# Two transformer layers on one core: the residual rows go to DRAM during the experts, the norm behind them goes tile by tile, and small products are joined

## The chip, the cores and the metric

The kernel runs on one core of a Trainium2 chip. Times are device microseconds of that core; the figure compared is the median over the runs. One execution was profiled, and all rows below are of that one. Engines are called TensorE (PE in the profile; its weight loads are PEld), VectorE (DVE), ScalarE (ACT), GpSimd (POOL) and SyncE (SP), which issues most loads from DRAM.

## The reference

512 tokens of width 1024 pass two layers in float32.

```
first layer:
  h = rmsnorm(x);  proj = h @ w_in  -> u, v_a, q, k, v_b
  y_a = u * spatial gating(v_a);  y_b = difference attention(q, k, v_b), 8 heads
  merged = sigmoid(gate_a) * (y_a @ w_up_a) + sigmoid(gate_b) * (y_b @ w_up_b)
  x = x + merged @ w_out
  t = rmsnorm(x) * norm2_g
  group and two of its experts for each token (4 groups of 8 experts, width 256)
  x = x + sum over the two chosen experts of c * (silu(t @ w1) * (t @ w3)) @ w2
second layer:
  h = rmsnorm(x) * norm_mix
  compressed, selected and window attention with gates; a convolution of 31 taps;
  attention to a memory of 256 tokens; three gated branches summed; x = x + merged @ w_out
  x = x + (silu(t @ w_gate) * (t @ w_up)) @ w_down,   t = rmsnorm(x) * norm_ffn
```

## The kernel before

**Products.** Most products are made three times, from a high and a low part of both operands (`split_to`, `mm3`, lines 313 to 315): high by high, high by low, low by high. Rounding to the high part is ACT's, the low part is DVE's. Weights come in blocks of 1 MB: loaded (`wraw`), split (`whi`, `wlo`, lines 303 and 304), used. The experts' products and the memory's take weights and operands unsplit (`mraw`, line 272).

**Order of the work.** A queue (`Dense`) holds the dense products in their order, with calls of other functions between them. A step makes one group of products; evacuations (`evac`) are put off to the next group. Other stages (the two attentions) call the queue for so many ns between their own steps. Loads are issued as far ahead as there are places: ring `w` has the two buffers `wraw`, and ring `m`, for the experts and the memory, has places that are granted and taken back by `grant`: eight of the ring `p`, three `q`, the buffers of `w`, `h` and `l` (2 each), `u` and `s`. The instructions of an engine are ordered by a scheduler from the program; inside `ordered(...)` an engine keeps the program's order. Each engine and SP's queue work in that order, so what waits holds up what is behind it.

**Start.** Four tiles of 128 tokens are normed (`norm_in`, line 439 is the product with root and gain), transposed and split (`lay_in`), two of them ahead of the first products.

**Output projection and router (500 to 580 us).** `w_out` comes in four blocks of 256 columns. After each half block `ev_x` adds to the residual rows `x1` (in the buffer `r0`, 16 KB a partition), multiplies the new rows with the gain on POOL (line 803), writes them to DRAM (`xg_d`) and sums squares. `lay_l` transposes and splits the rows, and `logits` multiplies them with the router's weights, high and low (36 columns). The router's chain of small DVE operations follows (lines 1124 to 1232); it ends with the index lists, by which `gather` reads each expert's rows from DRAM.

**Experts (580 to 812 us).** 16 pairs of experts, each with room for 64 tokens. `lay_x` transposes the gathered rows (one half copied by ACT, one by DVE), `push_up` makes the products with w1 and w3 (line 923), `lay_h` the gating, `push_down` the product with w2 (line 943), which is scattered by token and choice to DRAM (`y_d`, line 949). The places are taken back near the end (pairs NP-5 and NP-4).

**Between the layers (812 to 860 us).** Three of four products for the memory's keys and values (line 997) remain. Four tiles `yk` of 1 MB are read from `y_d`, added to `x1` (line 1359), normed for two tiles at a time (squares on ACT, line 1365, ten small DVE steps, product with root and gain, line 1370), transposed and split (`lay_xn`); tiles 2 and 3 are laid between the two halves of the first block of weights. `x1` goes to DRAM (`x2_d`), from where it comes back at the end of the layer.

**Second layer.** The small products that matter here: the compression (`push_cmp`, 2 x 2 blocks of 24 products, 64 columns high and low apart), the gates (`push_gate`, 24 products of 24 columns), and in the sparse attention the products with the compressed values (line 1685), whose probabilities are transposed to 32 rows (line 1704).

Of the kernel before, what the change touches and what calls it, by code (L numbers as in the profile page):

```python
# [6 lines left out]
F32 = mybir.dt.float32  # L7
# [5 lines left out]
OP = mybir.AluOpType  # L13
# [9 lines left out]
RING = 8  # L23
# [136 lines left out]
def _body(ctx, tc, I, out):  # L160
# [4 lines left out]
    def sub(stack, name, bufs=1, side="left", **kw):  # L165
# [11 lines left out]
          "back": {"p": [f"p{i}" for i in range(RING)], "q": [f"q{i}" for i in range(RING2)], "s": ["s0"], "u": ["U"],  # L177
# [181 lines left out]
    def rsqrt(dst, ss, shape, scale, eps, pause=None, after=None):  # L359
# [15 lines left out]
        dve.scalar_tensor_tensor(dst, a, 0.703952253 * 2.38924456 * z, dst, op0=OP.add, op1=OP.mult)  # L375
# [3 lines left out]
        dve.scalar_tensor_tensor(dst, a, 0.703125, dst, op0=OP.add, op1=OP.mult)  # L379

# [44 lines left out]
    xs_in = {}  # L425

# [6 lines left out]
    def norm_in(t):  # L433
# [4 lines left out]
        rsqrt(rr, ss, [128, 1], 1.0 / D, EPS, after=eye)  # L438
        dve.scalar_tensor_tensor(y, xn[:, t], rr, gain, op0=OP.mult, op1=OP.mult)
# [28 lines left out]
    def constants(kp):  # L468
# [37 lines left out]
        pool.affine_select(wsn, wsn, pattern=[[0, 8], [-1, 128]], compare_op=OP.is_ge, fill=0.0, base=0,  # L506
# [51 lines left out]
    with ordered(nc.sync.engine, nc.scalar.engine):  # L558
# [18 lines left out]
        norm_in(3)  # L577
# [212 lines left out]
    xg_d = tc.dram_tile([S, D], F32, name="xg_d")  # L790
# [4 lines left out]
    def ev_x(c, q, ps):  # L795
# [4 lines left out]
        if q == 0:  # L800
            R["xg", c] = R["rt"].tile([128, 4, 256], F32, name="xg", tag="row")
        xg = R["xg", c][:, 2 * q:2 * q + 2]
        pool.tensor_mul(xg, xs, R["g2"][:, cs][:, None, :].to_broadcast([128, 2, 256]))
# [7 lines left out]
        if q:  # L811
            (pool if c == 3 else act).dma_start(xg_d.rearrange("(t p) d -> p t d", p=128)[:, :, cs], R["xg", c])
# [12 lines left out]
    def logits(c, q):  # L825
# [14 lines left out]
    def wo_amid(c):  # L840
        dn.flush()
        lay_l(c, 0)

    def wo_step(c):
        if c:
            logits(c - 1, 1)
        grant((2, 2, 2, 0)[c])

    for c in range(4):
        dense_N(w_out[:, c * 256:c * 256 + 256], 0, 256, lambda: mT, lambda _, q, ps, c=c: ev_x(c, q, ps),  # L850
                between=(lambda c=c: wo_between(c)) if c else None, amid=(lambda c=c: wo_amid(c)) if c else None)
# [15 lines left out]
    def gather(p):  # L867

        pool.indirect_dma_start(out=R["xe"][p % 2], out_offset=None, in_=xg_d,
# [1245 lines left out]
```

## Time and profile before

| | us |
|---|---|
| median of 3 runs | 1728.38 (1727.83 to 1731.09) |
| profiled execution | 1730.11 |
| its span | 1728.4 |
| TensorE busy | 1667.7 (96% of the span) |
| DVE, ACT, POOL busy | 890.9, 650.1, 269.5 |

A row of the timeline gives start, duration, engine, line, operation, output and inputs; equal neighbours are merged (x5), and the duration is then that of all. What stands in square brackets is idle time of the engine ahead of it and what ended it. Products overlap one another on TensorE: the pace is the distance of their starts, not their duration.

### The profile page before, as it was taken

The numbers are of one execution on the slowest core, as the hardware profiler recorded it, in microseconds if no ns is written. First come the engines' busy times: TensorE is split into PE (matmuls) and PEld (weight loads), VectorE is DVE, ScalarE is ACT, GpSimd is POOL, SyncE is SP. The second block draws the span as 40 slices with busy tenths as digits, with TensorE's granted clock in tenths as the row PEclk, the third lists the DMA queues.
The fourth block names the chain that finished last, engine by engine and source line by source line (L and its number), as shares of the span: only waits on it lengthen the run. The fifth ranks groups of instructions, "written<-read, shape, count | busy, mean of one in ns | idle before, by whom it ended". The sixth has DMA issues, their size and how long they took to land.

```text
span 1728.4 us, 24549 instructions
## 1 busy us (share of the span) xinstructions
PE 1667.7 (96%) x9802; PEld 1361.1 (79%) x9802; DVE 890.9 (52%) x1958; ACT 650.1 (38%) x1127; POOL 269.5 (16%) x266
## 2 busy tenths in 40 slices
PE   8999999999999899888899999999999999999999
PEld 8988899998789655455789877777779888888887
DVE  7642358887653412010778755645995544444221
ACT  4221235545523122111435487787433322222111
POOL 2000001101112222111100045454101011111000
PEclk9999999999999999999899999999999999999999
DMA  6323333133458999999434322222243233332241
GB/s 213 98 74 122 122 98 98 53 96 98 152 159 317 355 419 402 422 416 389 179 98 122 122 64 77 86 68 74 91 153 110 74 97 97 98 97 98 70 137 37
DMA packets 146859, 265.98 MB, mean 154 GB/s; under 512 B 11707, under 2 KB 113798, under 8 KB 134198
## 3 DMA queue, kind: packets, MB, share of 16 engines
q1 hardware_dynamic: 128598, 228.42, 36.9%
q0 software_dynamic: 11184, 27.41, 5.3%
q10 hardware_dynamic: 6960, 8.56, 1.4%
q8 instruction: 78, 1.28, 0.3%
q14 instruction: 39, 0.32, 0.1%
HBM read 248.62 MB, written 18.87 MB: 155 GB/s over the span
## 4 chain that ended last, share of the span: by engine, by line
PE 75%; DVE 9%; DMA 8%; ACT 4%; issue 2%; POOL 0%; ACTq 0%; SPq 0%; DVEq 0%; POOLq 0%
PE pd L313 19%; PE pd L315 19%; PE pd L314 18%; DMA mraw<-in_w 4%; PE pd L923 4%; PE pa L396 3%; PE pa L314 2%; PE pa L315 2%; PE pa L313 2%; DMA y_d<-yt,dest 2%; PE pd L943 2%; DVE wlo L304 2%; ACT whi L303 1%; PE pa L1717 1%; PE pa L1699 1%
## 5 line engine op out<-in xcount | busy, mean ns | idle before, releaser
L304 DVE TENSOR_TENSOR wlo<-wraw,whi 128x2048 fp32r<-128x2048 f32 (+3 forms) x113 | 246.4, 2180 | 202.7 <-ACT whi L303 197.5
L303 ACT ACTIVATE whi<-wraw 128x2048 fp32r<-128x2048 f32 (+3 forms) x126 | 213.1, 1697 | 350.0 <-PE pd L314 213.7
L314 PE MATMUL pd<-wlo,hT 128*128 128x256 f32 x512 | 144.5, 282 | 0.7 <-DVE wlo L304 0.5
L313 PE MATMUL pd<-whi,hT 128*128 128x256 f32 x512 | 144.9, 283 | 0.3 <-ACT hT L253 0.2
L315 PE MATMUL pd<-whi,hT 128*128 128x256 f32 x512 | 144.1, 281 | 0.0
L315 PE MATMUL pd<-hnT,wlo 128*128 128x512 f32 x352 | 139.4, 396 | 0.0
L313 PE MATMUL pd<-hnT,whi 128*128 128x512 f32 x352 | 139.3, 396 | 0.0
L314 PE MATMUL pd<-hnT,whi 128*128 128x512 f32 x352 | 139.2, 395 | 0.0
L923 PE MATMUL pd<-mraw,xs 128*64 128x256 f32 x1024 | 122.1, 385 | 17.1 <-DMA mraw<-in_w 16.9
L923 PEld LDWEIGHTS pd<-mraw,xs 128*64 128x64 f32 x1024 | 75.2, 138 | 62.5 <-DMA mraw<-in_w 21.2
L313 PE MATMUL pd<-xnT,whi 128*128 128x512 f32 (+1 forms) x280 | 112.4, 401 | 0.0
L315 PE MATMUL pd<-xnT,wlo 128*128 128x512 f32 (+1 forms) x280 | 111.1, 397 | 0.0
L314 PE MATMUL pd<-xnT,whi 128*128 128x512 f32 (+1 forms) x280 | 110.9, 396 | 0.0
L314 PEld LDWEIGHTS pd<-wlo,hT 128*128 128x128 f32 x512 | 96.8, 189 | 1.7 <-DVE wlo L304 0.7
L313 PEld LDWEIGHTS pd<-whi,hT 128*128 128x128 f32 x512 | 96.8, 189 | 1.1 <-ACT hT L253 0.5
L315 PEld LDWEIGHTS pd<-whi,hT 128*128 128x128 f32 x512 | 96.7, 189 | 0.0
L1826 POOL TENSOR_TENSOR oa<-oa,ctm 128x512 f32<-128x512 f32 x60 | 77.5, 1291 | 99.0 <-ACT ctm L1825 97.1
L891 DVE SCALAR_TENSOR_TENSOR sg<-sg,pd 128x256 f32<-128x256 f32 x16 | 6.7, 421 | 161.1 <-ACT sg L890 161.1
L314 PEld LDWEIGHTS pd<-hnT,whi 128*128 128x128 f32 x352 | 66.1, 188 | 16.1
L313 PEld LDWEIGHTS pd<-hnT,whi 128*128 128x128 f32 x352 | 66.1, 188 | 15.8
L315 PEld LDWEIGHTS pd<-hnT,wlo 128*128 128x128 f32 x352 | 66.1, 188 | 15.8
L313 PE MATMUL pd<-hT,whi 128*128 128x512 f32 x192 | 76.7, 399 | 0.0
(521 smaller groups left out, 3879.2 us busy)
## 6 DMA issues: line engine op xcount, KB each, us to landing
mraw<-in_w SPq DMA_DIRECT2D x96, 1024.0 KB
wraw<-in_w_in SPq DMA_DIRECT2D x43, 1024.0 KB
wraw<-in_w_gate SPq DMA_DIRECT2D x19, 1024.0 KB
wraw<-in_w_up SPq DMA_DIRECT2D x11, 1024.0 KB
wraw<-in_w_down SPq DMA_DIRECT2D x10, 1024.0 KB
wraw<-in_w_out SPq DMA_DIRECT2D x8, 1024.0 KB
wraw<-in_w_up_a SPq DMA_DIRECT2D x4, 1024.0 KB
qk<-qk POOLq DMA_DIRECT2D x16, 256.0 KB, 6.4
```

The source lines that it names most:

```text
L303: act.activation(h[:, sl], r[:, sl], AF.Copy)
L304: (pool if i in by_pool else dve).tensor_tensor(l[:, sl], r[:, sl], raw(h[:, sl]), op=OP.subtract)
L313: pe.matmul(ps, ah, bh, start=start, stop=False)
L314: pe.matmul(ps, ah, bl, start=False, stop=False)
L315: pe.matmul(ps, al, bh, start=False, stop=stop)
L396: pe.transpose(ps[:, t * 128:t * 128 + 128], src_of(t), ident)
L891: dve.scalar_tensor_tensor(sg, sg, 1.0, hid[:, 0:256], op0=OP.add, op1=OP.mult)
L923: pe.matmul(ph[64 * m:64 * m + 64, 256 * j:256 * j + 256], XS[p][:, k, 64 * m:64 * m + 64], w[:, k], start=k == 0, stop=k == 7)
L943: pe.matmul(py[64 * q:64 * q + 64], hs[:, k, own], wt[:, k, 512 * q:512 * q + 512], start=k == 0, stop=k == 1)
L1699: pe.matmul(po[g, qt][64 * x:64 * x + 64], v, p, start=first, stop=last)
L1717: pe.matmul(ps[:, :nm], Q[:, 4 * g + i, qs], KS[:, br, g, x, :nm], start=x == 0, stop=x == 1)
L1826: pool.tensor_add(acc, acc, tm)
```

## The change

- The residual rows, not multiplied with the gain, are written to DRAM (`x1_d`) block by block where `xg_d` was written; the gain is applied by DVE at the transposes of the gathered rows (`lay_x`).
- The buffer `r0` is then room for two more loads ("x"), and the ring `p` has nine places. The buffers of `w` are granted after the third block of `w_out`. The experts' results have three buffers for four, the gated rows one for two.
- Behind the experts the rows are read back (`x1b`), and each tile of 128 tokens is added, squared and normed for itself (`norm_x`): POOL multiplies with the gain, and the root comes in as a diagonal matrix at the transposes. Tile 0 comes ahead of the first products, the others between them. One split of weights fewer comes ahead of it.
- Side by side: the router's weights, high and low in one operand of 100 columns, the compression's blocks in 128, the gates' weights in 56; two products for three, and the halves are summed by a product with stacked identities or by DVE. The compressed probabilities are padded to 128 columns, the compressed values to 128 rows.
- At the start the inverse roots follow one another, and a POOL operation on the spatial weights is put behind the last norm.

```diff
-RING = 8
+RING = 9
@@ ring_tile
+        if at == "x":
+            if "x" not in MR:
+                MR["x"] = r0.tile([128, 2, 8 * 256], F32, name="xroom", tag="r0")
+            return MR["x"][:, tag].rearrange("p (a b) -> p a b", a=shape[1])
@@ dense_N
-                        if q and i and amid:
-                            amid()
+                        if i and amid:
+                            amid(q)
@@ norm_in
-        rsqrt(rr, ss, [128, 1], 1.0 / D, EPS, after=eye)
+        order["rs"] = rsqrt(rr, ss, [128, 1], 1.0 / D, EPS, after=order["rs"])
...
-        norm_in(3)
+        behind(order["wsn"], norm_in(3))
@@ ev_x
-        xg = R["xg", c][:, 2 * q:2 * q + 2]
-        pool.tensor_mul(xg, xs, R["g2"][:, cs][:, None, :].to_broadcast([128, 2, 256]))
...
-            (pool if c == 3 else act).dma_start(xg_d.rearrange("(t p) d -> p t d", p=128)[:, :, cs], R["xg", c])
+            (pool if c == 3 else act).dma_start(x1v[:, :, cs], x1[:, :, cs])
@@ logits
-            mm3(R["lgp", q][0:36, 0:256], R["wrh"][:, k], R["wrl"][:, k], xT[0][:, j], xT[1][:, j],
-                k == 0, k == 7)
+            for x in range(2):
+                pe.matmul(R["lgp", q][0:100, 0:256], R["wrx"][:, k], xT[x][:, j], start=k + x == 0, stop=k + x == 8)
@@ wo_step
+        if c == 2:
+            dn.room["w"] = 0
+            grant(2, "w")
@@ lay_x
-            if q:
-                dve.tensor_copy(xs[:, 4:8], p3)
-            else:
-                act.activation(xs[:, 0:4], p3, AF.Copy)
+            ks = slice(4 * q, 4 * q + 4)
+            dve.tensor_mul(xs[:, ks], p3, R["g2k"][:, ks, None].to_broadcast([128, 4, 128]))
@@ lay_h, push_down: sg bufs 2 -> 1, yt bufs 4 -> 3
@@ experts, p == NP - 4
-            dn.call(lambda: (grant(-RING2, "q"), grant(-1, "s")))
+            dn.call(lambda: (grant(-RING2, "q"), grant(-1, "s"), grant(-2, "x")))
@@ router, after the copies of the logits
+        grant(2, "x")
         dn.prepare(2)
         lgq = psa()
         for t in range(4):
-            pe.transpose(lgq[:, t * 36:t * 36 + 36], lgT[:, t * 128:t * 128 + 128], ident[0:36, 0:36])
+            pe.matmul(lgq[:, t * 36:t * 36 + 36], lgT[:, t * 128:t * 128 + 128], halves2r[0:100], start=True, stop=True)
...
-        pool.dma_start(R["g2"], bc(I["norm_mix_2"], 0, [[0, 128], [1, D]]))
@@ between the layers
     dense_N(w_in2, 2328, 256, lambda: xnT, lambda c, q, ps: ev_qm(c, q, ps),
-            between=lambda: (lay_xn(2), lay_xn(3)))
+            between=lambda: norm_x(2), amid=lambda q: norm_x(3 if q else 1))
...
-    dn.prepare(5)
+    dn.prepare(4)
...
+    x1 = r0.tile([128, 4, D], F32, name="x1b", tag="r0")
+    for t in range(4):
+        sync.dma_start(x1[:, t], x1v[:, t])
+    yk = []
+    for tag in "KQ":
+        y2 = br_p.tile([128, 2, 2, D], F32, name="yk", tag=tag)
+        for i in range(2):
+            yk.append(y2[:, i])
+            sync.dma_start(y2[:, i], yv[:, 2 * (tag == "Q") + i])
+    gx = half("C", "gx", F32)[:, 0:2].rearrange("p a b -> p (a b)")
+    act.dma_start(gx, bc(I["norm_mix_2"], 0, [[0, 128], [1, D]]))
+    dgx = half("D", "dgx", F32)
...
+    def gains(t):
+        act.activation(yk[t][:, 0], x1[:, t], AF.Square, accum_out=nss[:, t:t + 1])
+        order["gx"] = pool.tensor_mul(yk[t][:, 1], x1[:, t], gx)
+
+    def factor(a, b):
+        rsqrt(nrr[:, a:b], nss[:, a:b], [128, b - a], 1.0 / D, EPS)
+        for t in range(a, b):
+            dve.tensor_scalar(dgx[:, t, 0:128], ident, nrr[:, t:t + 1], None, op0=OP.mult)
+
+    def norm_x(t):
+        if t == 0:
+            add_row(0, 0)
+            add_row(0, 1)
+            gains(0)
+            add_row(1, 0)
+            factor(0, 1)
+            add_row(1, 1)
+            gains(1)
+            add_row(2, 0)
+            add_row(3, 0, pool)
+        elif t == 1:
+            factor(1, 2)
+            add_row(2, 1)
+            add_row(3, 1)
+            gains(2)
+            gains(3)
+        elif t == 2:
+            factor(2, 4)
+        ts_ = slice(t * 128, t * 128 + 128)
+        for hf in range(2):
+            ps = transpose4(lambda k: yk[t][:, 1, (4 * hf + k) * 128:(4 * hf + k) * 128 + 128], diag=dgx[:, t, 0:128])
+            ks = slice(4 * hf, 4 * hf + 4)
+            split_to(xnT[0][:, ks, ts_], xnT[1][:, ks, ts_], ps.rearrange("p (k s) -> p k s", k=4))
...
+    with ordered(nc.vector.engine):
+        norm_x(0)
+        dn.step()
+        dn.step()
+    for t in range(4):
+        pool.dma_start(x2_d[:, t], x1[:, t])
@@ push_cmp
-                    mm3(cm["ps"][0:64, 256 * a:256 * a + 256], BH[a][:, 0, jj], BH[a][:, 1, jj], wt[0][:, j], wt[1][:, j],
-                        jj == 0, jj == 15)
+                    for x in range(2):
+                        pe.matmul(cm["ps"][:, 256 * a:256 * a + 256], BH[a][:, jj].rearrange("p x i -> p (x i)"),
+                                  wt[x][:, j], start=jj + x == 0, stop=jj + x == 16)
@@ cmp_gelu
-        act.activation(x, cm["ps"][0:64], AF.Copy)
+        act.activation(x, cm["ps"][64:128], AF.Copy)
+        dve.tensor_add(x, x, cm["ps"][0:64])
@@ push_gate
-                mm3(ps[0:24], wt[0][:, k], wt[1][:, k], xnT[0][:, k], xnT[1][:, k], k == 0, k == 7)
+                for x in range(2):
+                    pe.matmul(ps[0:56], wt[:, k], xnT[x][:, k], start=k + x == 0, stop=k + x == 8)
@@ cmp_turn_
-            ps = transpose4_32(sc)
-            hl = [t2("pt").bitcast(F32R)[0:32] for _ in range(2)]
-            split_to(hl[0], hl[1], ps[0:32])
+            ps = transpose4(lambda i: sc[:, i])
+            hl = [t2("pt").bitcast(F32R) for _ in range(2)]
+            split_to(hl[0], hl[1], ps)
```

## Rows read from the trace of the kernel before

**Rows 1.** The page's first part: busy us, share, instructions of each engine.
```profile
PE 1667.7 (96%) x9802; PEld 1361.1 (79%) x9802; DVE 890.9 (52%) x1958; ACT 650.1 (38%) x1127; POOL 269.5 (16%) x266
```
**Rows 2.** Stretches: us, busy of PE, PEld, DVE, ACT, POOL; clock, DMA share, GB/s.
```profile
540.00:550.00 10.00, 10.00 (x87) 9.96 (x87) 2.08 (x3) 2.90 (x10) 2.53 (x2) 1.00 0.77 288
550.00:560.00 10.00, 9.93 (x85) 9.58 (x84) 3.17 (x6) 2.34 (x8) 2.34 (x3) 1.00 0.42 133
...
570.00:580.00 10.00, 6.37 (x78) 5.82 (x78) 7.78 (x27) 0.32 (x2) 3.29 (x4) 1.00 0.78 300
580.00:590.00 10.00, 9.76 (x86) 6.47 (x86) 3.78 (x15) 1.58 (x3) 1.95 (x2) 1.00 0.79 293
...
720.00:730.00 10.00, 7.79 (x55) 4.25 (x52) 0.95 (x2) 2.06 (x4) 3.04 (x3) 1.00 1.01 421
...
840.00:850.00 10.00, 7.30 (x33) 6.65 (x32) 8.54 (x20) 4.25 (x8) 2.06 (x5) 0.50 0.30 118
```
**Rows 3.** Waits of SP's DMA queue, 500 to 850: total us, times, longest.
```profile
SPq L272 <- PE pd L315: 20.6, 2, 12.9
SPq L272 <- DVE vals L1223: 17.7, 1, 17.7
```
**Rows 4.** Timeline between the experts and the second layer.
```profile
820.85 2.56 SPq L1345 DMA_DIRECT2D yk<-y_d  x4
...
828.22 6.01 DVE L1359 TENSOR_TENSOR x<-x,yk 128x1024 f32<-128x1024 f32 x5
...
838.98 3.65 PE L396 MATMUL pa<-ident,ny 128*128 128x128 f32 x16 [5.71 <-issue]
...
845.32 0.58 PE L313 MATMUL pd<-whi,xnT 128*128 128x256 f32 x1 [2.69 <-ACT xnT L253]
```
**Rows 5.** Timeline of DVE and POOL, at the start and at the router.
```profile
8.79 2.48 DVE L439 SCALAR_TENSOR_TENSOR ny<-xn,nrr,gain 128x1024 f32<-128x1024 f32 x2
...
19.28 1.05 DVE L374 SCALAR_TENSOR_TENSOR rs_a<-rs_a,rs_v 128x1 f32<-128x1 f32 x1
...
559.87 1.29 POOL L803 TENSOR_TENSOR xg<-x,gain 128x512 f32<-128x512 f32 x1
...
560.40 1.68 DVE L366 TENSOR_SCALAR rs_v<-s 128x4 f32<-128x4 f32 x1
```
**Rows 6.** TensorE's waits over the span: total us, times, longest.
```profile
PE pd L923 <- DMA mraw<-in_w: 16.9, 9, 3.0
...
PE pa L396 <- DVE ny L439: 3.7, 2, 2.5
...
PE pa L314 <- DVE xT L822: 1.9, 1, 1.9
...
PE pa L1500 <- DVE cu L1494: 1.1, 1, 1.1
```
**Rows 7.** TensorE's timeline: a logits group to the next product; a compressed value pair.
```profile
545.00 0.28 PE L313 MATMUL pa<-xT,wrh 128*36 128x256 f32 x1
...
545.70 0.28 PE L313 MATMUL pd<-whi,mT 128*128 128x256 f32 x1
...
1056.69 0.73 PE L1685 MATMUL pa<-pt,vcs 32*128 32x512 f32 x2
1057.35 0.39 PE L1717 MATMUL pa<-KS,Q 128*128 128x256 f32 x1
```
**Rows 8.** DMA issues: count, KB each, median us from issue to landing.
```profile
xg_d<-xg POOLq DMA_DIRECT2D x1, 512.0 KB, 8.9
...
y_d<-yt,dest POOLq DMA_INDIRECT x32, 7.5
```
**Rows 9.** Timeline of SP's queue, 545 to 560.
```profile
545.07 14.96 SPq L272 DMA_DIRECT2D mraw<-in_w  x5
```
**Rows 10.** Stretches of the compression's products (24) and of the gates' (24 and 3 more).
```profile
923.55:926.43 2.88, 2.88 (x24) 2.78 (x24) 0.00 (x0) 0.00 (x0) 1.00 0.01 3
...
887.20:892.75 5.55, 5.55 (x27) 2.52 (x24) 5.50 (x7) 2.52 (x7) 0.00 (x0) 1.00 0.02 3
```

More of the change, by code (lines that the diff above doesn't have):

```diff
@@ L176, in _body @@
     MR = {"free": deque(), "owed": {}, "at": {},
-          "back": {"p": [f"p{i}" for i in range(RING)], "q": [f"q{i}" for i in range(RING2)], "s": ["s0"], "u": ["U"],
+          "back": {"p": [f"p{i}" for i in range(RING)], "q": [f"q{i}" for i in range(RING2)], "s": ["s0"], "u": ["U"], "x": [0, 1],
                    "w": ["wraw0", "wraw1"], "h": ["whi0", "whi1"], "l": ["wlo0", "wlo1"]}}
@@ L425, in _body @@
     xs_in = {}
+    order = {"rs": eye}
     def warm(n):
@@ L1103, in _body @@
     pool.memset(ones, 1.0)
+    halves2r = rt.tile([128, 36], F32, name="halves2r")
+    pool.memset(halves2r, 0.0)
+    for at in (0, 64):
+        pool.tensor_copy(halves2r[at:at + 36], ident[at:at + 36, at:at + 36])
     grant(RING - 6)
@@ L1111, in _body @@
     grant(RING2, "q")
-    dn.room["w"] = 0
-    grant(2, "w")
     grant(2, "h")
@@ L1127, in _body @@
         lg = tmp("lg", 4, 36)
[L1128 removed]
+        lgT = rt.tile([100, S], F32, name="lgT", tag="jk", bufs=2)
         for q in range(2):
[L1130 removed]
+            act.activation(lgT[:, 256 * q:256 * q + 256], R["lgp", q][0:100, 0:256], AF.Copy)
+        grant(2, "x")
         dn.prepare(2)
@@ L1353, in half @@
         return (p or br_p).tile([128, 4, S], dtype, name=name, tag=tag)
-    ny = [half(tag, "ny", F32).rearrange("p (a k) s -> p a (k s)", a=2) for tag in "CD"]
-    with ordered(nc.vector.engine):
-        def add_rows(t, ks=(0, 1)):
-            for k in ks:
-                dve.tensor_add(x1[:, t], x1[:, t], yk[t][:, k])
-        for q in range(2):
-            ss, rr = small("nss", [128, 2], 4), small("nrr", [128, 2], 4)
-            for t in (2 * q, 2 * q + 1):
-                add_rows(t, (1,) if t == 2 else (0, 1))
-                act.activation(ny[q][:, t % 2], x1[:, t], AF.Square, accum_out=ss[:, t % 2:t % 2 + 1])
-            if q == 0:
-                add_rows(2, (0,))
-            rsqrt(rr, ss, [128, 2], 1.0 / D, EPS)
-            for t in range(2):
-                dve.scalar_tensor_tensor(ny[q][:, t], x1[:, 2 * q + t], rr[:, t:t + 1], R["g2"], op0=OP.mult, op1=OP.mult)
+    x1 = r0.tile([128, 4, D], F32, name="x1b", tag="r0")
@@ L1395, in _body @@
     kcT = na.tile([128, 2, 2, 32], F32R, name="kcT")
-    vcs = na.tile([32, 2, 2, 64], F32R, name="vcs")
+    vcs = na.tile([128, 2, 2, 64], F32R, name="vcs")
+    pool.memset(raw(vcs), 0.0)
+    scz = [na.tile([128, 4, 128], F32, name=f"scz{i}") for i in range(2)]
+    for z in scz:
+        pool.memset(z, 0.0)
     cmask = na.tile([128, 512], F32, name="cmask")
@@ L1460, in ev_blk @@
     def ev_blk(a, ps):
-        pool.memset(blk[a][:, :, :, 31:32], 0.0)
+        behind(pool.memset(blk[a][:, :, :, 31:32], 0.0), order["gx"])
         for g in range(2):
@@ L1549, in lay_kv, with side @@
             pool.dma_start(KS[other, br, g], KS[own, br, g])
+    halves2 = p2.tile([128, 24], F32, name="halves2")
+    behind(pool.memset(halves2, 0.0), order["gx"])
+    for at in (0, 32):
+        pool.tensor_copy(halves2[at:at + 24], ident[at:at + 24, at:at + 24])
     def push_gate():
         v = w_in2.rearrange("(k p) c -> p k c", p=128)
+        load, split = wtile([(lambda r: r, v[:, :, 1280:1304])], (128, 8, 24))
+        both = p2.tile([128, 8, 56], F32R, name="gboth")
+        behind(pool.memset(raw(both), 0.0), order["gx"])
+        def side(r):
+            h, l = split(r)
+            act.activation(both[:, :, 0:24], raw(h), AF.Copy)
+            act.activation(both[:, :, 32:56], raw(l), AF.Copy)
+            return both
         def g(wt):
@@ L1699, in gather_values @@
                 pe.matmul(po[g, qt][64 * x:64 * x + 64], v, p, start=first, stop=last)
-        def transpose4_32(sc):
-            ps = psa()
-            for i in range(4):
-                pe.transpose(ps[0:32, i * 128:i * 128 + 128], sc[:, i], ident)
-            return ps
         def scores(u, hf, cps):
@@ L1882, in ev_g1 @@
         act.activation(Qb["g1"][:, j], ps, AF.Tanh, scale=0.5)
-    for t in range(4):
-        pool.dma_start(x2_d[:, t], x1[:, t])
-    lay_xn(0)
-    lay_xn(1)
     dn.call(lambda: lay_qm(0))
```

87 lines of the change are left out of this document (40 added, 47 removed).

## The prediction

> **What bounds the kernel now.** I read the busy shares first: TensorE is busy for 96% of the span [rows 1], so in most places only fewer products can shorten it. Then the stretches of 10 us, with the DMA's share beside TensorE's. The reader is to see two gaps in the DMA's work ahead of the experts (0.77 and 0.42 of full from 540 to 560, 0.78 and 0.79 from 570 to 590), and behind them a DMA at 1.01 while TensorE drops to 7.79 of 10 us [rows 2]. The experts run from 580 to 812, and there the weights bound the kernel, not the products: whatever is loaded in the gaps needn't be loaded later. Third, the waits of SP's DMA queue, which say why the gaps are there: no place is free. It waits 20.6 us in two waits for the last products that read old buffers, and 17.7 us for the router to end [rows 3]. Fourth, the timeline between the experts and the second layer: TensorE has been idle for 5.7 us when the transposes of the normed rows start at 838.98, and for 2.7 more when the first product on them starts at 845.32 [rows 4], and the granted clock there is 0.50 [rows 2], the 1.2 GHz level.
>
> **The change, part by part.** Durations are from the profiled execution, which took 1730.11 us (span 1728.4). That is 1.7 us above the median of the runs, 1728.38, so the sum comes off 1730.11 and then 1.7 us more for the median.
>
> *Start.* The inverse roots of the first two row tiles, now interleaved, run one behind the other, so the first norm can start before 8.79; a POOL operation on the spatial weights goes behind the last norm, where a small step of DVE now takes 1.05 us [rows 5]. TensorE waits 3.7 us there in two waits [rows 6]. Between nothing and 3.7 I take 1.5, because the first wait then meets the split of the weights. **-1.5.**
>
> *Router logits.* Three products for each of 16 (column block, half, k) become two, high and low weights side by side in 100 columns. Six go from 545.00 to 545.70 [rows 7], 0.117 us each: 16 x 0.117 = **-1.9**, in a stretch where TensorE is full [rows 2]. The rows now go to DRAM as they are, so POOL's products with the gain go, 1.29 us each; the last of them ran beside the router's first step, which took 1.68 us [rows 5], and TensorE then waited 1.9 us for its next operand [rows 6]. Between 0 and 1.9 I take 1.0, since two POOL fills of the gather's buffers stay. **-1.0.** The gain is applied where the experts' rows are transposed: both halves are then DVE's instead of one ACT's, some 0.7 us more in a pair of experts, and a pair lasts 14.5 us (232 over 16). DVE is nearly empty there (0.95 of 10 us [rows 2]) and the first products need only the first half: nothing. Without that cover it is 16 x 0.7 = 11 us.
>
> *Three more places for weights (one in the ring, two in the room of the residual rows).* Each holds 1.05 MB; at the 421 GB/s of the experts' stretch [rows 2] that is 2.5 us. Free ahead of the experts are 2.3 + 5.8 = 8.1 us in the first gap and 2.2 + 2.1 = 4.3 in the second [rows 2]. The ring's place falls into the first. The room opens when the last store of the rows has landed: that takes 8.9 us [rows 8] from about 559.9, when POOL now starts its last product [rows 5], so at about 569. The five loads that go out from 545.07 on [rows 9] are 12.5 us of DMA and are still landing then; the room's two, 5 us, go into the second gap, which also loses the 0.5 MB of the second layer's gain. Filled: 3 x 2.5 = 7.5 us. Bounds: 2.5 (only the ring's place pays) and 7.5. I take the upper one, since the second gap is about as large as what goes in and the DMA sets the experts' end (from 720 to 730 TensorE is idle for 2.2 us [rows 2], and its longest wait in total is for these weights, 16.9 us [rows 6]). **-7.5.**
>
> *What the places cost.* One buffer less for the experts' results (3 for 4) and for the gated rows (1 for 2). The one reader of the gated rows stands ahead of their next writer: nothing. A result's buffer comes round after one and a half pairs, some 21 us, against 7.5 us to landing [rows 8]; only the last four stand closer, and y is late behind them for another reason, as follows.
>
> *Behind the experts.* Now: y is read from 820.85, five sums run from 828.22, and one chain for two tiles leads to 845.32, 17.1 us later [rows 4]; of the 7.3 us of products at half clock from 840 to 850 [rows 2] half, 3.7, is lost. New: 2 MB of rows are read again and 0.5 MB of gain is loaded late, 2.6 MB or 6 us in front of y in a queue that is full. But the first sum now waits for a split of weights and not for y (no idle is shown ahead of it [rows 4]), and that split moves behind; y's first tile, 2.5 us of DMA from 820.85, can have been there by some 825. So it is some 3 us late against 828.22, and its chain is short: two sums (2.4), square (1.25), ten small steps (2.0), diagonal (0.2), transposes and first copy (1.5), about 8 us instead of 17. The first product comes some 6 us earlier. Then tiles 1 to 3 wait each for its own factor, with a square and a sum ahead of it on ACT and DVE, 1 to 3 us each, where there is no wait now. Between -6 (ACT copies ahead of its squares) and +6 (each tile waits 4 us, the clock stays low) I take **-1.5**, nearer to neither. The rows' stores to DRAM come later, and nothing waits for them.
>
> *Small products side by side.* The compression goes from 96 products to 64: 24 take 2.88 us [rows 10], so 32 x 0.12 = -3.8. The gates go from 24 to 16: 24 take 5.55 us [rows 10], so -1.85. The 16 value products with 32 rows get 128: such a pair takes 0.66 us from its start to the next product [rows 7], against 0.46 at the gates' pace, so 8 x 0.2 = -1.6 (bounds 0 and 2.3). One sum more in the compression's activation lies on a chain for which TensorE already waits 1.1 us [rows 6]: +0.7. TensorE is full around all of these. **-6.5.**
> The rows show that a product of 36 columns starts at the usual pace behind one of 128 [rows 7]. The Trainium skill (TensorEngine Tiling (Array Packing), Key Properties) says that changing the tiling mode drains the engine. By that rule the narrow products would pay at each entry, and widening them would give some 15 x 0.2 = 3 us more; the trace agrees for the products of 32 rows and not for those of 36 columns, so the sum leaves it out.
>
> Sum: -1.5 - 1.9 - 1.0 - 7.5 - 1.5 - 6.5 = -19.9, so 1710.2 for an execution like the profiled one and **1708.5** for the median.
>
> **The rivals.** *B. POOL and DVE get into each other's way behind the experts.* Four products with the gain and one sum are POOL's now, of 1024 columns, twice the 1.29 us of 512: 12.9 us in all, and a small step of DVE beside such an operation took 1.68 us [rows 5]. If 9.5 us of it come to lie on the norms' chain, that part is +8 and the time 1718. For it: the chain steps from DVE to POOL and back. Against it: the tiles overlap.
> The Trainium skill (SBUF — State Buffer, SBUF: two separate sides) says that the port pair of DVE and POOL is locked for a whole instruction. The trace agrees at 560.40 [rows 5]; by that rule this case is a mechanism and no mishap.
> *C. The room opens late, or its loads slow the first gathers of rows*, which share the DMA: only the ring's place pays, and the experts start some 2 us later: 1708.5 + 5 + 2 = 1715.5. For it: the gathers come just when the gap is filled.
> *D. The side-by-side products give nothing*, since DVE ends last around them: 1708.5 + 6.5 + 1.9 = 1717. Against it: TensorE's waits there are small.
> *E. Slower.* SP's loads are one queue in order. If a load into the residual rows' room stands ahead of the five from 545.07 on [rows 9], it waits for the rows' store until 569, and they with it. The DMA is then idle for 24 us against 8.1, and the 7.5 are gone: 1708.5 + 16 + 7.5 = 1732. It decides at one point, the order of SP's queue at 545. Against it: the room is granted late in the router, behind other places.
>
> **How the numbers follow.** A, as summed, 55%, own range 1702 to 1715; B 20%, C 12%, D 5%, E 8%. 0.2% is 3.5 us, about what a measurement can tell from no change here. Faster by more: A, C, D and most of B, 0.87; within: B's tail and part of E, 0.06; slower: most of E, 0.07. The range takes A with both ends of the norms' term, B, C and D: 1698 to 1722.
>
> **What would show it.** Right: a DMA share above 0.9 in nearly all of 545 to 590; the last expert's product about 12 us earlier, near 800; 32 logit, 64 compression and 16 gate products at the same paces; under 8 us of idle TensorE from the memory's products to those of the last tile. Wrong: a long wait of SP for the rows' store (E); DVE steps of over 1 us beside POOL's products behind the experts (B); the experts' end less than 8 us earlier (C); TensorE waiting for DVE or ACT from 900 to 1220 (D).

## The result, and the profile after

The changed kernel takes **1740.43 us** (median of 4 runs, 1739.82 to 1741.59) against 1729.23 for the kernel before on the same chip: ratio 1.0064, 95% interval 1.0049 to 1.0079. It is 11.2 us slower, where 19.9 us faster was forecast. In the profiled executions the span went from 1728.4 to 1738.1.

TensorE's record has 16 instructions fewer, and yet it is busy 5 us longer, and the span is 10 us longer [rows 1]. The 16 are a balance: the joined products are 56 fewer, but the 32 transposes behind the experts, made with the diagonal as ordinary products, are recorded as 64, and the four products that sum the halves in the router and the four at the gates as 8 each:

```profile
PE 1672.6 (96%) x9786; PEld 1368.9 (79%) x9786; DVE 903.2 (52%) x1984; ACT 642.4 (37%) x1113; POOL 274.5 (16%) x273
```

The stretches that answer to [rows 2], with the ones behind them:

```profile
540.00:550.00 10.00, 10.00 (x87) 10.00 (x86) 1.72 (x3) 1.92 (x8) 0.00 (x0) 1.00 1.02 389
550.00:560.00 10.00, 9.68 (x84) 9.46 (x83) 3.20 (x6) 2.36 (x8) 1.12 (x2) 1.00 0.55 183
...
570.00:580.00 10.00, 6.32 (x78) 5.77 (x77) 7.70 (x26) 0.31 (x2) 3.42 (x4) 1.00 1.01 422
580.00:590.00 10.00, 8.33 (x54) 6.03 (x55) 4.09 (x15) 0.00 (x0) 0.99 (x1) 0.66 0.49 165
720.00:730.00 10.00, 10.00 (x74) 5.62 (x72) 2.19 (x4) 1.95 (x4) 3.04 (x3) 1.00 1.01 423
830.00:840.00 10.00, 1.03 (x5) 0.57 (x3) 7.87 (x15) 1.75 (x3) 7.82 (x12) 0.80 0.99 386
840.00:850.00 10.00, 8.60 (x48) 8.46 (x49) 7.99 (x17) 2.31 (x4) 6.20 (x3) 0.69 0.25 102
850.00:860.00 10.00, 6.05 (x45) 5.28 (x44) 6.85 (x16) 3.89 (x8) 7.83 (x10) 1.00 0.26 105
...
870.00:880.00 10.00, 7.25 (x48) 6.83 (x47) 9.83 (x31) 3.44 (x4) 0.00 (x0) 0.83 0.17 30
```

The gaps in the DMA's work are filled from 540 to 550 and from 570 to 580, most of the one from 550 to 560 stays (0.55 busy, 0.42 before), and the next one, from 580 to 590, has become larger (0.49, 0.79 before). In the stretch of the experts from 720 to 730 TensorE no longer waits. Behind the experts it is nearly idle from 830 to 840, and then idle again for 4.0 us of the stretch from 850 and 2.8 of that from 870: three holes where there was one.

The timeline through these holes answers to [rows 4] (start, duration, engine; idle time ahead in square brackets):

```profile
818.57 9.02 SPq L1366 DMA_DIRECT2D yk<-y_d  x4
821.35 2.29 DVE L308 TENSOR_TENSOR wlo<-wraw,whi 128x2048 fp32r<-128x2048 f32 x1 [19.83 <-ACT whi L307]
822.21 1.91 ACT L307 ACTIVATE whi<-wraw 128x2048 fp32r<-128x2048 f32 x1 [0.89 <-DMA wraw<-in_w_in]
831.75 4.08 DVE L1373 TENSOR_TENSOR x1b<-x1b,yk 128x1024 f32<-128x1024 f32 x3 [8.10 <-DMA yk<-y_d]
836.17 2.34 POOL L1378 TENSOR_TENSOR yk<-x1b,gx 128x1024 f32<-128x1024 f32 x1
836.38 2.15 DVE L377 TENSOR_TENSOR rs_a<-nrr 128x1 f32<-128x1 f32 x1
839.73 0.29 DVE L1383 TENSOR_SCALAR dgx<-ident,nrr 128x128 f32<-128x128 f32 x1
840.22 3.75 PE L403 MATMUL pa<-dgx,yk 128*128 128x128 f32 x16 [9.19 <-DMA wraw<-in_w_in]
841.23 3.28 POOL L1378 TENSOR_TENSOR yk<-x1b,gx 128x1024 f32<-128x1024 f32 x1 [2.14 <-DVE x1b L1373]
845.80 1.67 DVE L377 TENSOR_TENSOR rs_a<-nrr 128x1 f32<-128x1 f32 x1
849.06 2.02 PE L403 MATMUL pa<-dgx,yk 128*128 128x128 f32 x16 [1.18 <-issue]
858.31 0.48 DVE L1383 TENSOR_SCALAR dgx<-ident,nrr 128x128 f32<-128x128 f32 x2
858.70 2.61 PE L403 MATMUL pa<-dgx,yk 128*128 128x128 f32 x16 [3.10 <-POOL blk L1504]
871.49 2.28 DVE L308 TENSOR_TENSOR wlo<-wraw,whi 128x2048 fp32r<-128x2048 f32 x1
873.82 0.58 PE L318 MATMUL pd<-wlo,xnT 128*128 128x256 f32 x1 [1.31 <-DVE wlo L308]
```

On the trace's time axis the first sum comes 3.5 us later than before. Counted from the last expert product, which comes 2.3 us earlier, it is 5.9 us later (23.5 us behind it, 17.7 before), where 3 was forecast. From there each tile takes some 9 us: transposes at 840.22, 849.06 and 858.70, each right behind its diagonal (`dgx`). And the high half of the second block's weights is ready by 824.12, but its low half waits behind the whole norm in DVE's written order, until 871.49.

TensorE's waits say the same [rows 6]: the wait for the experts' weights fell from 16.9 to 7.9 us. One for the gated rows grew from 2.8 to 5.8, that for the low halves of weights from 0.7 to 4.1, and two at the transposes with the diagonal are new. The view puts these two down to a load and to a POOL fill; in the timeline above it is the tile's diagonal that ends just ahead of each.

```profile
PE pa L403 <- DMA wraw<-in_w_in: 9.2, 1, 9.2
PE pd L928 <- DMA mraw<-in_w: 7.9, 5, 2.2
PE pa L401 <- DVE sg L897: 5.8, 1, 5.8
PE pd L318 <- DVE wlo L308: 4.1, 4, 1.4
PE pa L403 <- POOL blk L1504: 3.1, 1, 3.1
```

### The profile page after: what moved, and what is told of

It is laid out like the page before. It is cut to its first block, busy times and chain, and to the rows that moved or that the text cites. A ratio compares the mean times of both kernels' runs of the same rounds, so it can differ in the third digit from the quotient of the medians.

```text
span 1738.1 us, 24531 instructions
## 1 busy us (share of the span) xinstructions
PE 1672.6 (96%) x9786; PEld 1368.9 (79%) x9786; DVE 903.2 (52%) x1984; ACT 642.4 (37%) x1113; POOL 274.5 (16%) x273
## 4 chain that ended last, share of the span: by engine, by line
PE 45%; DVE 3%; ACT 2%; DMA 2%; POOL 0%; issue 0%; SPq 0%; ACTq 0%
PE pd L317 12%; PE pd L318 12%; PE pd L319 12%; PE pa L318 2%; PE pa L317 2%; PE pa L319 2%; PE pa L401 2%; PE pa L1774 1%; DMA wraw<-in_w_in 1%; DVE wlo L308 1%; PE pa L1762 1%; ACT whi L307 1%; PE pa L403 0%; DMA gx<-in_norm_mix 0%; ACT ctm L1882 0%
## 5 line engine op out<-in xcount | busy, mean ns | idle before, releaser
L317 PE MATMUL pd<-xnT,whi 128*128 128x512 f32 x272 | 109.1, 401 | 0.0
L319 PE MATMUL pd<-xnT,wlo 128*128 128x512 f32 x272 | 107.9, 397 | 0.0
L318 PE MATMUL pd<-xnT,whi 128*128 128x512 f32 x272 | 107.7, 396 | 0.0
L319 PEld LDWEIGHTS pd<-hnT,wlo 128*128 128x128 f32 x352 | 66.1, 188 | 15.9
L318 PEld LDWEIGHTS pd<-hnT,whi 128*128 128x128 f32 x352 | 66.1, 188 | 15.9
```

Of the source, the lines that this page charges most:

```text
L317: pe.matmul(ps, ah, bh, start=start, stop=False)
L318: pe.matmul(ps, ah, bl, start=False, stop=False)
L319: pe.matmul(ps, al, bh, start=False, stop=stop)
```

## The experiments

The table gives for every kernel the ratio to the kernel before with its 95% interval, and, from its profiled execution, the us between marks of TensorE: *logits* from the first product on mT to the last of the logits; *router* to the first expert product; *experts* to their last; *memory* to the last product of the memory's keys and values; *block 1* to the 96th product on the normed rows; *block 2* to the 192nd; *rest* to the last product of all.

| kernel | ratio (interval) | logits | router | experts | memory | block 1 | block 2 | rest |
|---|---|---|---|---|---|---|---|---|
| before | 1 | 58.1 | 16.9 | 229.8 | 22.7 | 28.4 | 11.2 | 851.7 |
| after | 1.0064 (1.0049 to 1.0079) | 56.5 | 22.1 | 222.7 | 22.8 | 39.1 | 16.3 | 847.2 |
| small | 0.9982 (0.9973 to 0.9990) | 57.1 | 17.7 | 229.3 | 22.8 | 28.5 | 11.2 | 848.3 |
| start | 1.0001 (0.9992 to 1.0010) | 58.1 | 17.1 | 230.4 | 21.4 | 28.4 | 11.2 | 851.3 |
| noroom | 1.0049 (1.0036 to 1.0063) | 56.7 | 18.9 | 227.6 | 21.4 | 38.3 | 16.4 | 847.3 |
| pairs | 0.9979 (0.9970 to 0.9988) | 56.7 | 21.8 | 223.9 | 22.5 | 28.7 | 11.2 | 848.4 |
| split5 | 1.0047 (1.0031 to 1.0062) | 56.4 | 22.5 | 222.3 | 22.9 | 38.9 | 11.2 | 848.6 |
| nogain | 1.0038 (1.0025 to 1.0050) | 56.6 | 21.9 | 222.7 | 22.8 | 31.9 | 18.7 | 847.6 |
| tilesdve | 1.0040 (1.0026 to 1.0054) | 56.7 | 21.8 | 223.2 | 22.7 | 34.0 | 17.0 | 847.3 |
| tilesdve5 | 1.0018 (1.0009 to 1.0027) | 56.7 | 21.3 | 223.0 | 22.8 | 31.5 | 11.3 | 849.7 |
| lateroom | 0.9963 (0.9951 to 0.9975) | 56.7 | 19.6 | 222.8 | 22.8 | 27.9 | 11.2 | 848.5 |
| ring9 | 0.9969 (0.9958 to 0.9981) | 56.7 | 18.8 | 227.1 | 23.0 | 25.9 | 11.2 | 848.3 |
| copyfirst | 0.9987 (0.9978 to 0.9996) | 56.7 | 18.6 | 224.9 | 22.8 | 34.1 | 11.2 | 848.4 |
| kept | 0.9958 (0.9944 to 0.9973) | 56.7 | 18.7 | 227.0 | 22.7 | 24.1 | 11.2 | 848.6 |

Ahead of *logits* the profiled executions differ by up to 3.5 us even between kernels with equal code up to there; that stretch is left out of the reading.

The table's second row already holds the bill of the change: -1.6 logits, +5.2 router, -7.1 experts, +0.1 memory, +10.8 and +5.1 for the two blocks behind them, -4.5 in the rest; with 1.2 ahead of them that is 9.2 of the 9.7 us of span.

**small.** On the kernel before, only the side-by-side products:

```diff
-            mm3(R["lgp", q][0:36, 0:256], R["wrh"][:, k], R["wrl"][:, k], xT[0][:, j], xT[1][:, j], ...
+            for x in range(2):
+                pe.matmul(R["lgp", q][0:100, 0:256], R["wrx"][:, k], xT[x][:, j], ...
...
```

> Only the small products side by side (logits, compression, gates, values), on the kernel before; all else as it was. Theory 1, they gain where the trace after shows it (logits 1.6, compression and gates 3.9, some of it given back before the keys): 5 to 6 us, so 1723 to 1725. Prediction's own terms would make it 8.4 less, 1721. Rival D, vector engine or scalar engine end last around them: 1727 to 1730, no change.

Measured: 0.9982, 3.1 us less (1.7 to 4.7). Faster, but half of the expected. The products are gone as counted (groups of lines in small, 874 to 1000: 64 compression products, 16 gate products at the old pace):

```profile
L1490 PE MATMUL pd<-whi,bhl 128*128 128x256 f32 x32 | 8.1, 287 | 0.0
L1490 PE MATMUL pd<-wlo,bhl 128*128 128x256 f32 x32 | 8.1, 290 | 1.6 <-DVE wlo L304 1.6
...
L1583 PE MATMUL pd<-xnT,gboth 128*56 128x512 f32 x16 | 3.8, 392 | 0.0
```

The wait at the end of the second row was 0.2 before: with less work for TensorE, the low halves of the next weights come too late. From the first product behind block 2's normed queries (874.32 before) to the first one behind the compression's activation (968.56 before) small gains 1.6 us of the 5.65 that the removed products are worth. TensorE's idle time in this stretch grew from 1.6 to 4.3 us; the waits for wlo grew from 0.2 to 2.8. The last 1.3 us were not traced. Rival D, given 5%, was partly right. The stretch from the first value product to the last is 1.6 us shorter, as forecast, the logits are 1.0; the router gives 0.9 back. The traces show where: the router's four transposes, which are products on 100 rows now, are recorded as 8 and take 1.75 us from the first to the end of the last, 0.85 before.

**start.** On the kernel before, only the order at the start:

```diff
-        rsqrt(rr, ss, [128, 1], 1.0 / D, EPS, after=eye)
+        order["rs"] = rsqrt(rr, ss, [128, 1], 1.0 / D, EPS, after=order["rs"])
...
-        norm_in(3)
+        behind(order["wsn"], norm_in(3))
```

> Only the order at the start changed (inverse roots one behind the other, the spatial weights' operation behind the last norm), on the kernel before. Prediction: 1.5 us less, 1727.5. Theory 1, from the trace after, in which the first yaT product comes 1.7 us later: 1.5 to 2 us more, 1731. Rival: that shift came with something else of the change, then no change.

Measured: 1.0001 (0.9992 to 1.0010): nothing, and neither the forecast's -1.5 nor theory 1. The rival of no change is what came. TensorE's waits for the norm did shrink, from 3.7 [rows 6] to 2.3 (0.74, 1.07 and a third of 0.52). But the first products then wait for the split, 1.4 us where it was 0.7:

```profile
9.23 1.09 PE L397 MATMUL pa<-ident,ny 128*128 128x128 f32 x8 [0.74 <-DVE ny L441]
11.39 1.09 PE L397 MATMUL pa<-ident,ny 128*128 128x128 f32 x8 [1.07 <-DVE ny L441]
14.00 0.58 PE L314 MATMUL pd<-wlo,hT 128*128 128x256 f32 x1 [1.40 <-DVE wlo L304]
```

**noroom.** The changed kernel without the two places in the room of the residual rows:

```diff
-            dn.call(lambda: (grant(-RING2, "q"), grant(-1, "s"), grant(-2, "x")))
+            dn.call(lambda: (grant(-RING2, "q"), grant(-1, "s")))
...
-        grant(2, "x")
```

> The changed kernel without the two places in the residual rows' room; the ring's ninth place and all else stay. Theory 1 (the room's loads slow the first gathers of rows, and give back later what they take): first expert product 3 to 5 us earlier than in the changed kernel, last one of the experts at the same time or up to 2 us later, total 1739 to 1742. Rival 1, the places pay in full: experts' end 5 us later, total 1745. Rival 2, the places only cost: experts' end 3 to 5 us earlier, total 1736.

Measured: 1.0049, which overlaps the changed kernel's interval: no difference is shown, as theory 1 says. The marks say how it cancels: the room costs 3.2 us in the router (22.1 against 18.9) and gives 5.0 in the experts. A caveat: with the room free, two of the four loads that read the rows back went out early, at 570.46 and 581.81.

**pairs.** The changed kernel with the norm by pairs of tiles, on DVE alone, and five weights prepared ahead; the rows are still read back and the gain loaded late:

```diff
-            between=lambda: norm_x(2), amid=lambda q: norm_x(3 if q else 1))
+            between=lambda: (lay_xn(2), lay_xn(3)))
...
-    dn.prepare(4)
+    dn.prepare(5)
...
-        order["gx"] = pool.tensor_mul(yk[t][:, 1], x1[:, t], gx)
+                order["gx"] = dve.scalar_tensor_tensor(yk[2 * q + t][:, 1], x1[:, 2 * q + t], rr[:, t:t + 1], gx, ...
```

> The changed kernel with the norm behind the experts by pairs of tiles as before, all of it on the vector engine (no gain products on GpSimd, no diagonal), five weights prepared ahead again, but the rows read back and the gain loaded late as in the changed kernel. Theory 1, the chain by single tiles costs most of the 16 us lost there (9 us for each tile, with small steps of 1.7 to 2.5 us beside GpSimd's products): the 96th product of the first block some 5 to 8 us earlier than in the changed kernel, total 1732 to 1735. Rival, the 2.6 MB in front of y are the price: first sum and total as in the changed kernel, 1739 to 1742.

Measured: 0.9979; some 14.7 us less than the changed kernel, more than theory 1 expected, and faster than the kernel before. So the loss sits in how the norm behind the experts was rebuilt; reading the rows back costs no more than pairs earns elsewhere. DVE's timeline in pairs shows both:

```profile
833.89 6.43 DVE L1371 TENSOR_TENSOR x1b<-x1b,yk 128x1024 f32<-128x1024 f32 x5 [5.26 <-DMA yk<-y_d]
...
844.77 2.35 DVE L1371 TENSOR_TENSOR x1b<-x1b,yk 128x1024 f32<-128x1024 f32 x2
847.04 0.68 DVE L258 TENSOR_TENSOR xnT<-pa,xnT 128x512 fp32r<-128x512 f32 x1
847.64 1.22 DVE L1371 TENSOR_TENSOR x1b<-x1b,yk 128x1024 f32<-128x1024 f32 x1
```

The first sum is 5.7 us later than before [rows 4], but a copy of the transposed rows here comes in between the second pair's sums. In the kernel before all three sums stood ahead of the copies, which began at 845.33, 5.3 us after the pair's products with the gain had ended at 840.07:

```profile
845.33 0.69 DVE L254 TENSOR_TENSOR xnT<-pa,xnT 128x512 fp32r<-128x512 f32 x1
```

From the first sum to the 96th product pairs takes 28.1 us, before 33.4: that pays for the late y.

Three runs take the rebuilt norm apart.

**split5.** The changed kernel with one line:

```diff
-    dn.prepare(4)
+    dn.prepare(5)
```

> The changed kernel with five weights prepared ahead again (the second weight's split stands in front of the norm's sums, where the vector engine idles for 8.1 us). Theory 1, the late split costs the 5.1 us that are lost between the 96th and the 192nd product: total 1735, and the 192nd product 5 us earlier. Rival, the norm's chain is what the second block waits for as well: no change, 1739 to 1741.

Measured: 1.0047; by the medians' ratios some 3 us less than the changed kernel, with overlapping intervals. The marks are clear: block 2 falls from 16.3 to 11.2, its value in the kernel before, and nothing else behind the experts moves; 1.4 of the 5.1 are given back in *rest*. Both splits now lie in DVE's idle time:

```profile
822.43 2.29 DVE L308 TENSOR_TENSOR wlo<-wraw,whi 128x2048 fp32r<-128x2048 f32 x1 [20.43 <-ACT whi L307]
825.07 2.29 DVE L308 TENSOR_TENSOR wlo<-wraw,whi 128x2048 fp32r<-128x2048 f32 x1 [0.34 <-ACT whi L307]
832.57 4.12 DVE L1373 TENSOR_TENSOR x1b<-x1b,yk 128x1024 f32<-128x1024 f32 x3 [5.20 <-DMA yk<-y_d]
```

**nogain.** The changed kernel without POOL's products with the gain (the gain is left out):

```diff
-        order["gx"] = pool.tensor_mul(yk[t][:, 1], x1[:, t], gx)
...
-            ps = transpose4(lambda k: yk[t][:, 1, (4 * hf + k) * 128:(4 * hf + k) * 128 + 128], ...
+            ps = transpose4(lambda k: x1[:, t, (4 * hf + k) * 128:(4 * hf + k) * 128 + 128], ...
```

> The changed kernel without the four products with the gain on GpSimd (the transposes read the rows themselves; the gain of the second layer's first norm is left out), all else the same, one row sum stays on GpSimd. Theory 1, GpSimd's products are what each tile waits for, by their own 2.3 to 3.3 us and by the small steps of 1.7 to 2.5 us beside them: each tile's step falls from 9 to about 6 us, 96th product 6 to 9 us earlier, total 1731 to 1734. Rival, the chain by single tiles is too long by itself: 0 to 3 us earlier, total 1737 to 1740.

Measured: 1.0038. Block 1 is 7.3 us shorter, in theory 1's range, and a tile's step is 7.3 (transposes at 837.55, 844.84, 852.15). But block 2, which still waits for the late split, is 2.3 us longer: by the medians' ratios 4.5 us remain, with intervals that just overlap, and the total lies between the two forecasts. The same small step, with no POOL operation of 1024 columns beside it, in nogain:

```profile
835.63 0.23 DVE L377 TENSOR_TENSOR rs_a<-nrr 128x1 f32<-128x1 f32 x1
843.13 0.16 DVE L377 TENSOR_TENSOR rs_a<-nrr 128x1 f32<-128x1 f32 x1
```

In the changed kernel it took 2.15 us beside the first of POOL's products and 1.67 beside the one row sum that POOL makes. That is rival B's mechanism, seen directly.

**tilesdve.** The changed kernel with the norm still tile by tile, but on DVE alone:

```diff
-        order["gx"] = pool.tensor_mul(yk[t][:, 1], x1[:, t], gx)
...
-            dve.tensor_scalar(dgx[:, t, 0:128], ident, nrr[:, t:t + 1], None, op0=OP.mult)
+            dve.scalar_tensor_tensor(yk[t][:, 1], x1[:, t], nrr[:, t:t + 1], gx, op0=OP.mult, op1=OP.mult)
```

> The changed kernel with the norm still by single tiles, but all of it on the vector engine (factor and gain in one operation, no diagonal, no GpSimd). Theory 1, the split over two engines is the price: 2.4 of sums, 2.0 of small steps, 1.25 of product and 1.4 of copies, 7 us for each tile against 9: 96th product 5 to 8 us earlier, total 1733 to 1736. Rival, single tiles against pairs are the price whatever engine does them: total 1738 to 1741.

Measured: 1.0040, some 4 us less than the changed kernel (the intervals just overlap), the upper end of theory 1. POOL's part, together with the diagonal, costs that much even where DVE has to do their work too. The edit takes out both: the transposes are ordinary ones again, 8 records for a tile and not 16. No run has the diagonal alone taken out; nogain, which keeps it, shows POOL's own part.

**tilesdve5.** tilesdve with five weights prepared ahead.

> The changed kernel with two things undone at once: the norm by single tiles wholly on the vector engine, and five weights prepared ahead. Theory 1, the two prices add (2.9 for the late split, 4.6 for GpSimd's part), and what is left against the norm by pairs, some 5 us, is the single tiles' own chain: total 1731 to 1733, from the memory's last product to the 192nd product of the layer about 45 us. Rival, they are one price counted twice: total 1735, 50 us. Second rival, single tiles cost nothing of their own: total 1727, 40 us.

Measured: 1.0018, 3.1 us above before (1.6 to 4.7). Block 2 is right again (11.3), so the prices of the late split and of POOL with the diagonal do add: 8 us of the changed kernel's loss. Against pairs, which differs only in pairs for tiles and the written order that goes with them, 6.7 us are left by the ratios; the marks of its profiled execution, which at 1727.25 lies 5.6 us below its median, show 2.8 (31.5 against 28.7 in block 1), with one wait for a tile's normed rows:

```profile
851.97 1.09 PE L401 MATMUL pa<-ident,yk 128*128 128x128 f32 x8 [1.83 <-DVE yk L1381]
```

So the single tiles have a price of their own, between 3 and 7 us; where the rest of it lies in the slower runs stays open.

**lateroom.** From pairs, with the old order at the start, and the room's two loads on POOL's queue behind the first two gathers:

```diff
-        grant(2, "x")
...
         gather(1)
+        grant(2, "x")
+        dn.load()
...
+                behind(pool.dma_start(r, src), order["gather"])
```

> The kernel with the norm by pairs (1726.5), the order at the start as before, and the two loads into the residual rows' room issued on GpSimd's queue behind the first two gathers. Theory 1, those loads delay the gathers by 3 us where they go out first: first expert product 3 us earlier, experts' end 1 to 3 us earlier, total 1723 to 1725. Rival, the weights bound the experts, and what the gathers gain the weights lose: total 1726 to 1728.

Measured: 0.9963, some 2.8 us less than pairs (the intervals just overlap). The router takes 19.6 instead of 21.8. In the changed kernel the transposes of the first rows waited for the gather issued at 576.29, and all six kernels with the room's loads in front spend 21.3 to 22.5 in the router; the three without the room, and the two with its loads behind the gathers, 18.6 to 19.6. Before, and then in the changed kernel:

```profile
574.78 1.13 POOL L869 DMA_INDIRECT xe<-xg_d,gidx  x1 [3.63 <-DVE gidx L1194]
579.32 1.45 PE L396 MATMUL pa<-ident,xe 128*128 128x128 f32 x10
...
569.59 0.80 SPq L276 DMA_DIRECT2D xroom<-in_w  x2
576.29 1.16 POOL L876 DMA_INDIRECT xe<-x_d,gidx  x1 [4.75 <-issue]
582.43 3.22 PE L401 MATMUL pa<-ident,xe 128*128 128x128 f32 x14 [1.67 <-DMA xe<-x_d,gidx]
```

**ring9.** lateroom without the room's two places.

> The kernel with the norm by pairs and the late room (1723.2), without the two places in the residual rows' room; the ring's ninth place stays. Theory 1, the room gives 3 to 4 us when its loads stay clear of the gathers: total 1726 to 1728, experts' end 3 to 4 us later. Rival, the room gives nothing, and the gathers alone made the difference: total 1723 to 1724. The prediction's term for the room was 5 us: 1728.

Measured: 0.9969, against 0.9963: no difference is shown, though by the intervals one of up to some 4 us could hide. The experts take 4.3 us more (227.1 against 222.8), but the first block takes 2.1 less, the router 0.8. This speaks for the rival that the room gives nothing, though not for the reason it gave. As in noroom, two loads of the rows went out early here.

**copyfirst.** lateroom, with the first pair's copies in front of the second pair's sums in DVE's order:

```diff
     with ordered(nc.vector.engine):
-        norm_rows()
+        norm_rows(0)
+        lay_xn(0)
+        lay_xn(1)
+        norm_rows(1)
```

> The kernel with the norm by pairs and the late room (1723.2), with the copies of the first pair's transposed rows in front of the second pair's sums on the vector engine. Theory 1, the first product waits for these copies and not for y: it comes 1.5 to 2 us earlier, total 1721 to 1722. Rival, the second pair then comes late by as much: total 1723 to 1724.

Measured: 0.9987, some 4 us more than lateroom: theory 1 falls, and the rival was too mild. The first product comes 13.3 us after the first sum, just as in lateroom, and then TensorE waits for the second pair:

```profile
840.44 3.64 PE L410 MATMUL pa<-ident,yk 128*128 128x128 f32 x16 [9.80 <-issue]
854.73 3.67 PE L410 MATMUL pa<-ident,yk 128*128 128x128 f32 x16 [4.00 <-DVE yk L1393]
```

What counts here is when the last tile is ready, not the first one.

**kept.** ring9 with the rows kept on the chip:

```diff
-    x1 = r0.tile([128, 4, D], F32, name="x1b", tag="r0")
-    for t in range(4):
-        sync.dma_start(x1[:, t], x1v[:, t])
```

> The kernel with the ring's ninth place, without the room (1725.3), and the residual rows kept on the chip behind the experts instead of read back: 2.1 MB less for the DMA in front of y. Theory 1, the first sum waits for a DMA that is full from 790 to 840, so it comes by 2.1 MB at some 400 GB/s, 5 us, earlier, until the splits in front of it end last: first sum 3 to 5 us earlier, total 1721 to 1723. Rival, the vector engine's splits and the memory's products end last there anyway: total 1725 to 1726.

Measured: 0.9958 (1722.08 us), the fastest of all, below the kernel before and 18 us below the changed one; from ring9 (0.9969) and lateroom it is not told apart. The total lies in theory 1's range. But the first sum is only 0.4 us earlier than in ring9 (1.9 counted from the last expert product): y's load was issued at 819.00, and then the second split stood in front of the sum, as the rival said.

```profile
819.00 2.09 SPq L1371 DMA_DIRECT2D yk<-y_d  x4
825.92 2.29 DVE L317 TENSOR_TENSOR wlo<-wraw,whi 128x2048 fp32r<-128x2048 f32 x1 [1.18 <-ACT whi L316]
828.13 6.01 DVE L1376 TENSOR_TENSOR x<-x,yk 128x1024 f32<-128x1024 f32 x5
```

In lateroom, whose experts end 3.3 us earlier, y was issued 2.7 us earlier and the sum yet began later, behind 2.1 MB of rows:

```profile
816.27 9.04 SPq L1376 DMA_DIRECT2D yk<-y_d  x4
828.89 6.43 DVE L1381 TENSOR_TENSOR x1b<-x1b,yk 128x1024 f32<-128x1024 f32 x5 [3.94 <-DMA yk<-y_d]
```

## Why the prediction was wrong

**Behind the experts, -1.5 forecast, +15.9 measured: the step that failed.** Three terms of it were wrong.

- The first product on the normed rows, forecast 6 us earlier, came 0.5 us later (12.6 us behind the memory's last product, 12.1 before). The first sum was late by 5.9 us and not by 3, counted from the last expert product; and the 8 us from there to the first product were 11.9. Of these the small steps took 3.9 (835.81 to 839.69) instead of 2.0, one of them beside POOL's product, and the transposes with the first copy 3.4 (840.22 to 843.62) instead of 1.5: with the diagonal a tile has 16 records on TensorE, where before 16 served two tiles [rows 4], and the sum had put the diagonal down as 0.2 us of DVE alone. The granted clock was low there too (0.69 from 840 to 850).
- "1 to 3 us" of wait for each of the tiles 1 to 3: from the first product to the 96th it is 26.5 us, 16.3 before, so 10.3 us for the three. The tiles' chains of some 9 us don't overlap. In the timeline DVE's order, which is written out, holds sums, small steps and copies of all tiles in one line: tile 1's square was done at 842.33, and its small steps began at 845.25, behind tile 0's copies. No run has single tiles without the written order, so how much of the price is the order's is not shown.
- The text said that the split of the second weight "moves behind", and cost it at nothing. It moved behind the whole norm, and block 2 lost 5.1 us (split5); the bounds of -6 and +6 left this out.

By runs: the late split some 3 us of time (split5), POOL with the diagonal some 4 (tilesdve), the single tiles 3 to 7 (tilesdve5 against pairs). One row could have warned: DVE was already the busiest engine there, 8.54 of 10 us [rows 2].

**Rival B** was the right mechanism. It wanted 9.5 us on the norms' chain; in nogain 7.3 us of block 1 go away, and 4.5 by time. The Trainium skill (SBUF — State Buffer, SBUF: two separate sides) says that the port pair of DVE and POOL is locked for a whole instruction; the small steps of 2.15 and 1.67 us that fall to 0.23 and 0.16 agree.

**Three places, -7.5.** The experts' stretch fell by 7.1, so the size was right, and it never reached the end. The last expert product came only 2.3 us earlier, rival C's sign. Some 3 us go back in the router, where the room's loads run ahead of the gathers (rival C, priced at 2). The rest goes back behind the experts, where the first sum is 5.9 us late against their end: y is issued some 10 us after the last expert product (10.3 before, 10.3 after, 10.0 in lateroom, 9.4 in kept), in a DMA that is full (1.02 to 1.08 of its time in each 10 us from 790 to 830 in the changed kernel), and reading the rows back takes as many bytes as the room had let in early. lateroom, ring9 and kept, three ways to trade the one for the other, are the same within their intervals. The ring's own place, with the earlier grant of two others, is worth 2 to 3 us in the experts (noroom, ring9 and kept against before and small).

**Router, -1.0 forecast, +5.2 measured.** 0.9 are the products in place of transposes (small), some 3 the room's loads ahead of the gathers. The remaining 1 also stands in the kernels without the room, and the traces of noroom, ring9 and kept place it: the first gather is issued 0.84 us after the index list is done, 0.29 before, and TensorE makes 14 transposes of gathered rows ahead of the first expert product, 10 before; these take 1.9 to 2.3 us, 1.45 before. Why the gather is issued later was not isolated. The removed POOL products gave 0.4: TensorE's wait fell from 1.9 to 1.5. The step that took 1.68 us beside the product [rows 5] still takes 1.32, for in both kernels it ends as a POOL fill of the gather's buffer ends (562.05 before, 561.66 after); the product was only part of what it waited for.

**Logits** -1.9 forecast, -1.6 measured (-1.0 in small): right. **Start** -1.5: the wait moved to the split; the doubt that the text had ("the first wait then meets the split") was the answer. **Small products** -6.5: the counts and paces were right, and so were the value products; of the 5.65 for compression and gates 4 did not come, and 2.7 of these are new idle time of TensorE, waits for the low halves of weights above all (small). The text let TensorE be "full around all of these" and didn't ask how far behind it DVE was. The Trainium skill's rule on the tiling mode (TensorEngine Tiling (Array Packing), Key Properties), by which the widened products would have given 3 us more, is not borne out for the products of 24, 36 and 64 columns: the counted products alone cover all that was gained. For those of 32 rows the trace of small agrees: where a transpose stands ahead of a value product, that product starts 0.03 us after it, 0.20 before.

**Rival E** did not come: SP did wait for the rows' store, 20.5 us in three waits up to 850, but behind the five loads; the DMA's share was 0.55 from 550 to 560 and near 1 around it, no 24 us of idle.

## What to carry to other kernels

Where an engine's order is written out, a step that an edit pushes behind that block can be late by as much as the block's length (here 5.1 us of it showed): list what is pushed behind, also the steps that belong to the next stage. A chain done in smaller pieces brings the first piece earlier and the last one later, and a consumer that needs all of them ends with the last. Room for early loads that must be bought back by reading the same bytes again later earned nothing that these runs could show, with the DMA full at both ends.

## What the runs showed that was not expected

A DVE step of one or two columns, 0.16 us alone, took up to 2.46 us beside a POOL product of 1024 columns (from 854.03 in the changed kernel), while two DVE sums of 1024 columns that overlap one kept their pace (2.35 for both, from 848.88 in the changed kernel) and POOL's product rose from 2.34 to 3.31. From the last expert product to the first load of y 9.4 to 10.3 us pass, of which the stores by index take 5.8 to land.
